# A longer booked duration for TensorE's rounded matmuls in a list scheduler's table: one layer of a hybrid Fourier, DeltaNet and ConvFFN backbone

## The chip, the cores and the metric

The kernel runs on one core of a Trainium2 chip. The core has five engines that run side by side, each with its own queue of instructions in a fixed order: TensorE (PE; its weight loads are shown apart as PEld), VectorE (DVE), ScalarE (ACT), GpSimd (POOL) and SyncE (SP), which issues all DMAs here. An instruction that depends on another engine's waits for a semaphore, and whatever stands behind it in its queue waits with it. The metric is the device time of one execution in microseconds (us), the median of several runs; lower is better.

## The reference

One layer, on 1024 latent tokens of 1024 channels with 256 context tokens, in float32:

```python
hc = modulate(rms_norm(ctx, norm_pre_mix[l]), csh1, csc1)
fc, oc, zc, gtc, ctx_states = mixer_core(hc, (zero, zero), w_in[l], ...)
hx = modulate(rms_norm(x, norm_pre_mix[l]), sh1, sc1)
fx, ox, zx, gtx, _ = mixer_core(hx, ctx_states, w_in[l], ...)
yx = merge_branches(fx, ox, zx, gtx, dn_norm[l], w_fourier[l], w_dn[l], w_out[l])
x = x + gt1 * rms_norm(yx, norm_post_mix[l])
x = ffn_sublayer(x, sh2, sc2, gt2, norm_pre_ffn[l], norm_post_ffn[l], w_up[l],
                 conv_ffn[l], w_down[l], rows, GRID_W)
```

`mixer_core` projects the tokens, applies a short depthwise convolution and SiLU to queries, keys and values, and runs a gated delta rule in chunks, forwards and backwards, for 8 heads of 128 channels; the context's final states start the latent pass. `merge_branches` takes a two-dimensional Fourier transform of 512 channels, gates both branches and projects them. `ffn_sublayer` is a ConvFFN of width 2816 with a 3x3 depthwise convolution on a grid 64 wide.

## The kernel before

**Arithmetic.** Every large product is computed from operands that are split into a rounded high part and a rounded remainder (type float32r, `F32R`): high by high, high by low, low by high (`product`, line 542). With a contraction of 1024 one half of a product, 128 rows by 512 columns, is 8 x 3 = 24 matmuls that accumulate in one PSUM bank. ScalarE makes a weight's high part and VectorE or POOL its remainder (`halves` and `split_over`, from line 526), after a DMA. Transposes and the delta rule's 128x128 products are plain float32.

**Stages.** First come the modulation rows (from `w_ada`), the pre-norms and transposes, then decay and beta. The delta-rule stage runs over ten parts, the heads x0 to x7 of the latent tokens and two groups of four context heads, c0 and c1 (`ORDER`, line 32). For each part it projects the query and convolves it (`kq_head`, `conv_taps` at line 743), forms decay products, inverts the 32x32 diagonal blocks of a triangular matrix row by row on VectorE (`invert_blocks`, line 837, 31 pairs of a multiplication and a subtraction), with round trips through DRAM, merges the blocks with small matmuls (`merge_blocks`, line 860) and scans over 8 chunks in both directions (`step`, `scan_head`). Projections that are due later (keys and values of the later heads, z, the branch gates, the Fourier input) are recorded beside them (`sides`, line 1186) with their own weight buffers and mostly one PSUM bank. Then come the Fourier transform, the remaining gates, the gated output, the projections `w_dn` and `w_fourier`, `w_out` with a norm, and the ConvFFN: `up_a` (line 1507) projects and convolves on VectorE, `up_u` projects and multiplies, `down` accumulates.

**Order.** None of this is issued as it is written. `record` (line 291) stores each operation with a booked duration from `cost` (line 247) and its dependencies; memory is laid out in fixed regions, so the reuse of a buffer or a bank is a dependency too (`gates`, line 323). `schedule` (line 351) then merges all of them once, before the program runs:

- An operation's rank is its booked duration plus the longest booked path behind it, plus a bonus that some operations have (`BON`, line 37), minus 0.1 (`MIX`) of the TensorE time booked for the operations recorded ahead of it (line 371).
- Each engine has a clock of its own in this plan. In each round the engine that can start first is taken; among its operations that are ready within 50 ns (`AHEAD`, line 27, used in line 410) the one of the highest rank is issued, and its end is its start plus the booked duration.
- A result reaches another engine after a booked latency (`LAT`, line 190, and `lat`, line 472: 200 ns from TensorE, 256 and 281 to it, 127 between two dependent operations of one engine other than TensorE, 1900 from a DMA).
- SyncE's DMAs have a booked transfer time and may run some 3 us ahead of it (`LEAD`, line 40). After a planned pause of over 3 us TensorE is booked at double durations for a while.

The order in which they come out is the order in which the instructions are written for all engines. On the chip the queues then run freely, held by semaphores alone. The booked durations decide nothing else. The profile puts nearly all instructions on line 349, the helper that issues them; groups are told apart by engine, operation and shape.

Of the kernel before, what the change touches and what calls it, by code (L numbers as in the profile page):

```python
# [10 lines left out]
F32R = mybir.dt.float32r  # L11
# [30 lines left out]
GR = T // GW  # L42


# [1 line left out]
def _groups(side):  # L46
    out, cur = [], None
    for tok in side.replace("(", " ( ").replace(")", " ) ").split():
        if tok == "(":
            cur = []  # L50
        elif tok == ")":
            out.append(cur)
            cur = None
        elif cur is None:
            out.append([tok])
        else:
            cur.append(tok)
    return out
# [130 lines left out]
class Program:  # L189
# [8 lines left out]
    def pool(self, name, bufs=1, space=None, side="left"):  # L198
        p = Pool(self, name, bufs, space, side)
        if space is None:  # L200
            self.events.append((True, p))
        return p
# [44 lines left out]
    def cost(self, eng, method, args, kw):  # L247
        out = args[0] if args else kw["out"]
        shape = out.shape
        n = math.prod(shape[1:])  # L250
        ins = [x for x in list(args[1:]) + list(kw.values()) if isinstance(x, View)]
        psum = any(v.slot.space == PSUM for v in ins)
        if eng == "PE":
            if method == "transpose":
                return max(53, args[1].shape[0] * 2 / 2.4 + 2)
            rhs, m = args[2], math.prod(args[1].shape[1:])
            n = max(math.prod(rhs.shape[1:]), m)
            if rhs.shape[0] <= 64 and m <= 64:
                return 34 if n <= 32 else 80
            return n / 2.4 + 3 if rhs.dtype == F32R and n >= 256 else n * 4 / 2.4 + 5  # L260
        if eng == "DVE":
            if method == "reciprocal":
                return 65 + 6.3 * n
            ptr = any(v.shape[-1] == 1 and v.arr.size <= P for v in ins) and method in ("tensor_scalar", "scalar_tensor_tensor")
            fast = method in ("tensor_copy", "tensor_scalar") and not psum and out.slot.space != PSUM
            return 66 + n / (1.92 if fast else 0.96) + (61 if ptr else 0)
        if eng == "ACT":
            aps = any(isinstance(kw.get(x), View) for x in ("scale", "bias", "accum_out"))
            return (51 if psum else 93) + n * 0.833 + (93 if aps else 0)
        if eng == "POOL":  # L270
            if method == "memset":
                return 36 + 0.83 * n
            if kw.get("op") == ALU.pow:
                return 300 + 165 * n
            if method == "tensor_copy":
                return 119 + 3.33 * n
            if method == "affine_select":
                return 1060
            return 140 + 2.12 * n
        run = 1  # L280
        view = out if isinstance(out, View) else args[1]
        if isinstance(view, View):
            a_ = view.arr
            for d in range(a_.ndim - 1, -1, -1):
                if a_.shape[d] > 1 and a_.strides[d] != run:
                    break
                run *= a_.shape[d]
        total = math.prod(shape) * 4
        return max(60.0, total / 359.0 * (1 if run * 4 >= 512 else 2))
# [192 lines left out]
def body(tc, a, out):  # L482
    prog = Program(tc)
    layer(prog, a, out)
    prog.run()


def layer(prog, a, out):
# [14 lines left out]
    def ps(tag, shape, name):  # L503
        return psum.tile(shape, F32, tag=tag, name=name, bufs=PPB if tag == "pp" else 1)
# [4 lines left out]
        rota[1] += 1  # L509
        return ps(rota[0][rota[1] % len(rota[0])], shape, name)  # L510

    # ---------------------------------------------------------------- constants
    prog.bonus = 2e5
    cc = cload("cc")
    ident = cload("ident", src=a["cst"][:, 0:128])
# [6 lines left out]
    po.memset(mhalf, -0.5)  # L522
    ve.tensor_scalar(convw, convw, 0.5, None, op0=ALU.mult)

    # ---------------------------------------------------------------- weights
    def halves(src, pl, tags, name, eng=None):
        n = src.shape[-1]
        h = pl.tile([P, n], F32R, tag=tags[0], name=f"h_{name}", bufs=WB[tags[0]])
        w = pl.tile([P, n], F32, tag=tags[1], name=f"w_{name}", bufs=WB[tags[1]])
        sp.dma_start(w, src)  # L530
        return h, split_over(pl, h, w, f"l_{name}", eng)
# [24 lines left out]
            (eng_h or ve).tensor_copy(h, src)  # L556
        (eng_l or ve).tensor_tensor(l, src, h.bitcast(F32), op=ALU.subtract)

    # ---------------------------------------------------------------- hidden states
    hx = pool("hx", bufs=1)  # L560

    dp = pool("delta", bufs=1, side="right")
# [6 lines left out]
    def dt(tag, name, shape=(P, T), dtype=F32):  # L569
        return dp.tile(list(shape), dtype, tag=tag, name=name, bufs=bufs.get(tag, 1))  # L570

    # ---------------------------------------------------------------- modulation, pre-norm
    prog.bonus = 2e5
    s = const.tile([P, KT, 2], F32, name="silu_c")
    th = dt("vt", "tanh_c", (P, KT, 2))
# [87 lines left out]
    def hxh(g):  # L663
        return lambda k: (hH[k][:, g * HALF:(g + 1) * HALF], hL[k][:, g * HALF:(g + 1) * HALF])

    # ---------------------------------------------------------------- decay and beta
    NCH = 10

    def small(name):
        return const.tile([P, 2, NH, NCH], F32, name=name)  # L670

    beta, ngc, eg, egl, etl = (small(n) for n in ("beta", "ngc", "eg", "egl", "etl"))
# [66 lines left out]
        for i in range(2):  # L739
            sp.dma_start(grd[80 * i:80 * i + 80, :], grs[:, i, :])  # L740

    # ---------------------------------------------------------------- conv of q, k, v
    def conv_taps(pt, acc, w3):
        n = acc.shape[-1]
        se.activation(acc, pt[:, 0:n], AF.Identity, scale=w3[:, 1:2])
        ve.scalar_tensor_tensor(acc[:, 1:n], pt[:, 0:n - 1], w3[:, 0:1], acc[:, 1:n], op0=ALU.mult, op1=ALU.add)
        ve.scalar_tensor_tensor(acc[:, 0:n - 1], pt[:, 1:n], w3[:, 2:3], acc[:, 0:n - 1], op0=ALU.mult, op1=ALU.add)
# [22 lines left out]
        ve.tensor_scalar(qn, squares(src, name, ("pd", "pd")), P * EPS, P * EPS * EPS, op0=ALU.mult, op1=ALU.add)  # L770
        return qn

    # ---------------------------------------------------------------- delta rule: preparation
    def coefs(name, rk, cols):
        b2 = const.tile([P, 2, 8], F32, tag="b2", name=f"b2_{name}", bufs=2)
        bk = const.tile([P, 2, 8], F32, tag="bk", name=f"bk_{name}", bufs=2)
        c1 = const.tile([P, 2, 8], F32, tag="c1", name=f"c1_{name}", bufs=2)
        rkb = rk.rearrange("p (o u) -> p o u", o=1).broadcast_to([P, 2, 8])
        ve.tensor_tensor(bk, cols(beta), rkb, op=ALU.mult)
        ve.tensor_tensor(b2, bk, rkb, op=ALU.mult)  # L780
        ve.scalar_tensor_tensor(c1, cols(eg), -1.0, rkb, op0=ALU.mult, op1=ALU.mult)
        return rk, b2, bk, c1
# [77 lines left out]
    def merge_blocks(name, LTs, bk, k2):  # L860
# [8 lines left out]
            po.tensor_copy(nb[bnd[b], :, bnd[b]], k1[bnd[b], NU:2 * NU, :])  # L869
        f1, f2 = k1[:, 0:NU, :], k2[:, 0:NU, :]  # L870
        b1, b2_ = k1[:, NU:2 * NU, :], k2[:, NU:2 * NU, :]
        # 32 -> 64
        pa = ps("pm", [P, NU, 32], f"pa_{name}")
        for u in range(NU):
            for q in range(2):
# [24 lines left out]
            te.matmul(pc[bnd[2], u, :], am[bnd[3], u, :], b2_[bnd[3], u, :], start=True, stop=True)  # L900
        ve.tensor_copy(Lf[bnd[1], :, bnd[0]], pc[bnd[1]])
        ve.tensor_copy(Lb[bnd[2], :, bnd[3]], pc[bnd[2]])
        # 64 -> 128
        pd_ = ps("pm", [P, NU, 64], f"pdd_{name}")
        for u in range(NU):
            te.matmul(pd_[lo64, u, :], Lf[hi64, u, lo64], nf[hi64, u, hi64], start=True, stop=True)
# [13 lines left out]

    sd_ = dram.tile([2, NH, P, P], F32, name="sdram")

    # ---------------------------------------------------------------- context pass
    def wi_k(h):
        return a["wi"][1 + 3 * h]

# [122 lines left out]
            for d in range(2):  # L1049
                sp.dma_start(sd_[d, 4 * p + hh], S[d])  # L1050

    # ---------------------------------------------------------------- latent pass
    od = dram.tile([NH, P, T], F32, name="od")
    zd = dram.tile([NH, P, T], F32, name="zd")
    rsd = dram.tile([NH, T], F32, name="rsd")
# [122 lines left out]
    @on_stage  # L1178
    def merge(i):
        co, _, fl = prep[i]  # L1180
        merged[i] = merge_blocks(stages[i][0], fl[1], co[2], blocks.pop(i))
# [53 lines left out]
            side("f", 2 * i - 16)  # L1235
            side("f", 2 * i - 15)

    # ---------------------------------------------------------------- Fourier branch
    ffd = dram.tile([NF, P, T], F32, name="ffd")
    QT = HALF // 2  # L1240
    waves = [dt("F", f"wave{e}", (P, 2, 2, QT)) for e in range(2)]
# [62 lines left out]
    close(dp)  # L1304
    rota[0] = ["pp", FBANK, "X0", "X1", "Y0", "Y1"]

    # ---------------------------------------------------------------- branch gates, gated delta output
    mp = pool("mH", bufs=17, side="right")

    def m_tile(p_, name, dtype=F32R):  # L1310
# [99 lines left out]
    close(yt)  # L1410
    close(ozp)

    # ---------------------------------------------------------------- merge of the branches
    lp = pool("mL", bufs=17, side="right")
    mH, mL = [[None] * 2 for _ in range(KT)], [[None] * 2 for _ in range(KT)]
    wop = pool("wo", bufs=1, side="right")
# [17 lines left out]
    close(gt)  # L1434
    close(fp)

    # ---------------------------------------------------------------- mixer output, second pre-norm
    x1d = dram.tile([T, D], F32, name="x1d")
    wp = pool("wp", bufs=2, side="right")
    g1r = wp.tile([P, D], F32, name="g1r", bufs=1)  # L1440
# [20 lines left out]
    for t in range(8):  # L1461
# [3 lines left out]
        n = 0  # L1465
# [23 lines left out]
    close(wp)  # L1489
    close(wop)  # L1490

    # ---------------------------------------------------------------- ConvFFN
    yp = pool("y2", bufs=1)
    y2 = [yp.tile([P, D], F32, name=f"y2_{t}") for t in range(8)]
    dwp = pool("wd", bufs=3)
# [156 lines left out]
```

## Time and profile before

| | |
|---|---|
| device time, median of 3 runs | 2151.86 us (2146.21, 2151.86, 2153.07) |
| span of the profiled execution | 2152.6 us; the profile shows no time of its own beside it |
| mean granted TensorE clock | 0.976 of full speed |
| idle time just before matmuls of the largest group | 106.2 us, of which 65.5 ended by DVE |
| DMA | 232.32 MB, mean 108 GB/s |

The span runs from the first to the last instruction. A group in the profile is one kind of instruction, with its output and input shapes, the number of its instructions, its busy time and the mean "duration" of one, and then the idle time of its engine just before them and what ended it. Matmuls are pipelined and their ends are modelled, so the mean duration of a matmul is more than its spacing in a dense stretch. The granted clock is the share of full speed that TensorE got; it falls where TensorE has stood idle.

### The profile page before, as it was taken

Reading aid. Unit: us, or ns where it says so; the run is one execution under the profiler, and the core shown is the slowest. Engines: PE = TensorE matmul, PEld = TensorE weight load, DVE = VectorE, ACT = ScalarE, POOL = GpSimd, SP = SyncE. Lnnn points to the kernel's source line nnn. Section 1 sums busy time; section 2 is a strip of 40 time slices with the busy share of each in tenths; the row PEclk is TensorE's granted clock in tenths of the full one; section 3 lists DMA queues with packets and bytes.
Section 4 is the critical chain, followed back from the end, with each engine's and each line's share of the span. In section 5 each row is a group of like instructions: output and inputs, shape, how many; then the busy total and the mean of one; then the engine's idle time right before and its main releaser. Section 6 shows DMA issues by size and latency. Waiting matters only on the chain. (4 is left out here: it accounts for less than half of the span.)

```text
span 2152.6 us, 31012 instructions
## 1 busy us (share of the span) xinstructions
PE 2023.2 (94%) x11734; PEld 1623.3 (75%) x11734; DVE 1378.7 (64%) x2608; ACT 740.5 (34%) x1740; POOL 486.8 (23%) x479
## 2 busy tenths in 40 slices
PE   6989999898979989999999999989999999999996
PEld 2777878786768777788777778768888888888885
DVE  7548767676677566653656492587465757475655
ACT  6365454453244433533421142422231222112212
POOL 4131121324233442441311000412010110101005
PEclk9999999899999999999999999989999999999998
DMA  7152323462342444332778561311111111111114
GB/s 274 47 190 83 105 84 126 130 195 66 97 134 84 120 128 114 101 105 76 230 251 292 165 220 42 105 40 44 40 59 35 54 49 45 50 45 50 49 49 147
DMA packets 164216, 232.32 MB, mean 108 GB/s; under 512 B 74097, under 2 KB 87250, under 8 KB 164066
## 3 DMA queue, kind: packets, MB, share of 16 engines
q1 hardware_dynamic: 164066, 230.34, 33.3%
q8 instruction: 92, 1.51, 0.3%
q14 instruction: 58, 0.48, 0.1%
HBM read 180.89 MB, written 49.40 MB: 107 GB/s over the span
## 5 line engine op out<-in xcount | busy, mean ns | idle before, releaser
L349 PE MATMUL p<-m,m 128*128 128x512 f32 (+5 forms) x11574 | 2009.4, 340 | 106.2 <-DVE m L349 65.5
L349 PEld LDWEIGHTS p<-m,m 128*128 128x128 f32 (+3 forms) x11574 | 1604.4, 174 | 501.6 <-ACT m L349 68.8
L349 POOL TENSOR_TENSOR m<-m,m 128x512 fp32r<-128x512 f32 (+6 forms) x244 | 380.5, 1572 | 1332.0 <-ACT m L349 532.6
L349 ACT ACTIVATE m<-m 128x512 fp32r<-128x512 f32 (+6 forms) x563 | 390.3, 711 | 775.0 <-DMA m<-in_wu_dram 254.4
L349 DVE TENSOR_TENSOR m<-m,m 128x512 fp32r<-128x512 f32 (+23 forms) x940 | 483.3, 521 | 192.7 <-ACT m L349 166.4
L349 DVE SCALAR_TENSOR_TENSOR m<-m,m,m 128x1024 f32<-128x1024 f32 (+2 forms) x260 | 304.2, 1176 | 37.8 <-DMA m<-in_w_ada_dram 24.4
L349 ACT ACTIVATE m<-p 128x128 f32<-128x128 f32 (+5 forms) x444 | 181.7, 427 | 336.9 <-PE p L349 309.2
L349 DVE SCALAR_TENSOR_TENSOR m<-p,m,m 128x128 f32<-128x128 f32 (+4 forms) x472 | 191.0, 442 | 110.3 <-ACT m L349 57.6
L349 ACT ACTIVATE m<-p,m 128x128 f32<-128x128 f32 (+2 forms) x240 | 115.6, 492 | 235.8 <-PE p L349 219.8
L349 DVE TENSOR_TENSOR m<-m,p 128x512 f32<-128x512 f32 (+3 forms) x229 | 123.8, 569 | 105.9 <-PE p L349 105.8
L349 DVE SCALAR_TENSOR_TENSOR m<-m,m 128x512 f32<-128x512 f32 (+6 forms) x141 | 107.0, 768 | 36.6 <-ACT m L349 29.1
L349 DVE COPY m<-p 32x256 f32<-32x256 f32 (+10 forms) x116 | 42.0, 367 | 64.0 <-ACT m L349 38.5
L349 POOL COPY m<-m 32x256 f32<-32x256 f32 (+2 forms) x136 | 53.6, 397 | 115.3 <-DMA m<-d 73.5
L349 DVE SCALAR_TENSOR_TENSOR m<-m,m,p 128x128 f32<-128x128 f32 x128 | 42.8, 342 | 41.5 <-PE p L349 40.2
L349 DVE TENSOR_SCALAR m<-m,m 128x1024 f32<-128x1024 f32 x44 | 35.2, 799 | 49.1 <-ACT m L349 36.0
L349 POOL MEMSET m<- 128x1024 f32 (+7 forms) x79 | 35.1, 456 | 134.9 <-PE p L349 101.6
L349 ACT ACTIVATE p<-p 128x128 f32<-128x128 f32 x208 | 55.3, 266 | 20.6 <-PE p L349 18.6
L349 DVE STREAM_TRANSPOSE m<-m 32x256 f32<-32x256 f32 (+1 forms) x50 | 24.5, 491 | 29.1 <-DMA m<-d 28.4
L349 DVE CAST m<-m 128x512 fp32r<-128x512 f32 (+3 forms) x45 | 26.3, 593 | 25.0 <-ACT m L349 23.4
L349 ACT ACTIVATION_READ_ACCUMULATOR p<-p 128x1 f32 x208 | 40.0, 192 | 0.0
L349 DVE TENSOR_TENSOR m<-p,m 128x512 f32<-128x512 f32 (+4 forms) x47 | 28.1, 608 | 11.9 <-PE p L349 11.7
L349 POOL TENSOR_SCALAR_AFFINE_SELECT m<-m 128x1024 f32<-128x1024 f32 x16 | 19.0, 1207 | 72.2 <-DVE m L349 72.2
(20 smaller groups left out, 130.4 us busy)
## 6 DMA issues: line engine op xcount, KB each, us to landing
m<-d SPq DMA_DIRECT2D x76, 512.0 KB
m<-d SPq DMA_DIRECT2D x114, 256.0 KB
m<-in_wi_dram SPq DMA_DIRECT2D x106, 256.0 KB
m<-in_w_ada_dram SPq DMA_DIRECT2D x48, 512.0 KB
d<-m SPq DMA_DIRECT2D x94, 256.0 KB
m<-in_wu_dram SPq DMA_DIRECT2D x88, 256.0 KB
m<-in_wn_dram SPq DMA_DIRECT2D x22, 512.0 KB
m<-in_x_dram SPq DMA_DIRECT2D x16, 512.0 KB
```

The source lines that it names most:

```text
L349: return getattr(engine.real, method)(*[real(v) for v in args], **{k_: real(v) for k_, v in kw.items()})
```

## The change

In `cost`, the booked duration of a TensorE matmul on rounded operands with 256 columns or more is longer: n/2.4 + 16 ns instead of n/2.4 + 3 for more than 256 columns, n/2.4 + 12 for 256. A plain float32 matmul is booked 1 ns longer. Nothing else is different but comment lines that became blank; all line numbers stay. What is computed, the instructions, the tiles, the buffers and the DMAs are the same, and `schedule` merges them anew with these numbers.

```diff
@@ -257,7 +257,7 @@
             n = max(math.prod(rhs.shape[1:]), m)
             if rhs.shape[0] <= 64 and m <= 64:
                 return 34 if n <= 32 else 80
-            return n / 2.4 + 3 if rhs.dtype == F32R and n >= 256 else n * 4 / 2.4 + 5
+            return n / 2.4 + (16 if n > 256 else 12) if rhs.dtype == F32R and n >= 256 else n * 4 / 2.4 + 6
         if eng == "DVE":
             if method == "reciprocal":
                 return 65 + 6.3 * n
```

## The prediction

> **What bounds the kernel now.** I read the page's head and its slices first, then the table of windows by stage, the chain of waits, TensorE's waits in the one stage that has many, and the timeline where the longest of them lie.
>
> ```profile
> span 2152.6 us, 31012 instructions
> PE 2023.2 (94%) x11734; PEld 1623.3 (75%) x11734; DVE 1378.7 (64%) x2608; ACT 740.5 (34%) x1740; POOL 486.8 (23%) x479
> ```
>
> TensorE (PE) is busy for 94% of the span, so 2152.6 - 2023.2 = 129.4 us are all that any order could win back from its idle time. The table of windows says where they lie; I cut it at the ends of the stages.
>
> ```profile
> 0.00:160.00 160.00, 130.59 (x639) 94.51 (x640) 97.77 (x180) 90.75 (x206) 54.16 (x54) 0.94 0.48 172
> 160.00:1000.00 840.00, 773.86 (x6271) 641.06 (x6270) 572.65 (x1586) 367.98 (x1058) 261.49 (x295) 0.97 0.37 110
> 1000.00:1380.00 380.00, 376.70 (x1655) 293.43 (x1654) 215.17 (x326) 106.67 (x204) 59.78 (x54) 1.00 0.55 185
> 1380.00:1440.00 60.00, 49.87 (x196) 36.53 (x195) 43.70 (x42) 18.92 (x27) 17.21 (x12) 0.89 0.16 54
> 1440.00:2123.00 683.00, 683.00 (x2940) 550.59 (x2939) 429.96 (x451) 150.93 (x230) 79.01 (x53) 1.00 0.15 49
> 2123.00:2153.00 30.00, 9.19 (x41) 7.17 (x39) 19.45 (x24) 5.24 (x16) 15.17 (x14) 0.69 0.50 175
> ```
>
> The columns after the length are busy time of PE, PEld, DVE, ACT and POOL, then the granted clock, the DMA share and GB/s. The loading of the first weights (0 to 160) leaves PE idle for 29.4 us, the delta-rule stage (160 to 1000) for 66.1 us, the start of the ConvFFN (1380 to 1440) for 10.1 us, the tail behind the last matmuls for 20.8 us. From 1440 to 2123 it is never idle. The clock was granted at 0.97 in the delta-rule stage, another 0.03 x 840 = 25 us at most. So about 66 + 25 = 91 us lie where an order has choices. The chain of waits gives the true spacing of the matmuls that the change books:
>
> ```profile
> 1655.63 100.66 PE p L349 x432
> 1756.30 100.43 PE p L349 x432
> ```
>
> 432 of them in 100.43 us are **232.5 ns** apiece, with nothing in between. The mean "duration" of the same group (below, 419 ns) overlaps its neighbours and isn't a spacing.
>
> **The change, part by part.** Line 260 books a rounded matmul of 512 columns at 512/2.4 + 3 = 216.3 ns; after it, at 512/2.4 + 16 = 229.3, 13.0 more. One of 256 columns goes from 109.7 to 118.7 (+9.0); a plain fp32 one gains 1 ns. No instruction is added, removed or reshaped: the 31012 stay, with their DMAs. What moves is the merge of the five queues.
>
> ```profile
> L349 PE MATMUL p<-m,m 128*128 128x512 f32 x1826 | 534.4, 419 | 22.8 <-DVE m L349 15.2 <-ACT m L349 6.8 <-ACT p L349 0.2
> L349 PE MATMUL p<-m,m 128*128 128x256 f32 x264 | 46.5, 303 | 4.4 <-DVE m L349 3.8 <-ACT m L349 0.4
> ```
>
> These are the groups of 160 to 1000. The plan's TensorE takes 1826 x 13.0 + 264 x 9.0 = 23.7 + 2.4 = 26 us longer over this stage than it did. On the chip nothing is longer. Two things change in line 351's merge. First the ranks: each half of a product (24 matmuls) on an operation's longest path raises it by 24 x 13.0 = 0.31 us, and the charge for lateness, 0.1 of the TensorE time recorded before it (line 371), grows as well. Only pairs of ready operations whose ranks lay that close change places. Second, the clock of the plan: at each product the other engines' operations seem ready earlier against TensorE than they did.
>
> Before, the plan's TensorE ran ahead of the chip's by 232.5 - 216.3 = 16.2 ns a matmul, 16.2 x 1826 = 29.6 us over the stage; after, by 232.5 - 229.3 = 3.2 ns, 5.8 us. **The change removes 23.8 us of this lag** of the chip behind its plan. What the lag does is seen in the engines that wait, in order, for PE's products (same window):
>
> ```profile
> DVE m L349 <- PE p L349: 112.0, 104, 4.4
> DVE m L349 <- ACT m L349: 87.0, 50, 7.7
> DVE m L349 <- DMA m<-d: 33.7, 12, 6.8
> DVE m L349 <- ACT p L349: 13.0, 6, 5.1
> DVE m L349 <- DMA d<-m: 4.2, 2, 3.9
> PE p L349 <- DVE m L349: 43.9, 34, 6.5
> PE p L349 <- ACT m L349: 12.6, 12, 4.8
> PE p L349 <- DMA m<-d: 6.1, 3, 5.3
> ```
>
> VectorE stands waiting 249.9 us, of which 112.0 (45%) for a matmul; what is queued behind the waiting instruction can't start, though its inputs may be there, and PE in turn waits 43.9 us for VectorE. A plan that has the end of a product right puts fewer such instructions too early. The gain lies between nothing (all lag hidden, since PE is busy for 92% of the stage) and the whole 23.8 us. I take VectorE's share: 0.45 x 23.8 = 10.7 us, an estimate.
>
> The other stages I cost at nothing. From 1440 on, PE is full and VectorE covers the rest with 430 of 683 us; if a conv came too late there, the nearest row is the wait at the ConvFFN's start, 4.94 us:
>
> ```profile
> 1427.14 3.32 PE L349 MATMUL p<-m,m 128*128 128x512 f32 x7 [4.94 <-DVE m L349]
> SPq L349 <- PE p L349: 1168.3, 266, 26.2
> ```
>
> That wait ends with the first conv and hangs on data; it stays, as do the loads at the start and the tail. SP's queue, too, is merged anew: its booked transfer times are unchanged, so in the plan loads come earlier against PE. On the chip most of them wait for PE to free a buffer (1168.3 us of waiting), which a booking doesn't hasten; the two or three buffers of each weight tag are the cover. If a load stood behind the wrong wait, the nearest row is PE's 5.28 us for a DMA, shown below; I take zero.
>
> By the Trainium skill ("TensorE: Matmul & The Clock Gate", section "Back-to-back issue gap") an isolated warm matmul of N columns is spaced N/2.4 + 2.5 ns, 215.8 for 512, and it gives some 131 as sustained. By either the old booking was right or long, and the new one is wrong by 13.5 ns or more. The trace disagrees with 232.5 ns over 864 matmuls.
>
> Sum: 2152.6 - 10.7 = 2141.9. The profile shows no time of that execution beside its span; the span lies 0.7 us over the median, 2151.86, well inside the runs (2146.21 to 2153.07), so I carry the difference over: 2151.86 - 10.7 = **2141** us.
>
> **The rivals.** *VectorE is planned too early (slower).* The longest wait of the delta-rule stage:
>
> ```profile
> 486.94 7.31 DVE L349 TENSOR_TENSOR m<-m,m 128x121 f32<-128x121 f32 x17
> 487.06 4.22 POOL L349 TENSOR_TENSOR m<-m,m 128x8 f32<-128x8 f32 x2 [0.98 <-DVE m L349]
> 491.52 0.67 ACT L349 ACTIVATE m<-p,m 128x512 f32<-128x512 f32 x1
> 494.28 2.87 DVE L349 TENSOR_TENSOR m<-m,m 128x30 f32<-128x30 f32 x4
> 497.07 0.74 DVE L349 SCALAR_TENSOR_TENSOR m<-p,m,m 128x511 f32<-128x511 f32 x1
> 498.74 3.75 PE L349 MATMUL p<-m,m 128*128 128x512 f32 x8 [6.52 <-DVE m L349]
> 480.00:500.00 20.00, 10.80 (x50) 8.27 (x51) 18.54 (x37) 12.24 (x40) 10.45 (x5) 0.91 0.34 118
> 500.00:520.00 20.00, 20.00 (x282) 15.23 (x282) 7.98 (x17) 6.73 (x13) 9.56 (x17) 0.92 0.34 97
> ```
>
> ScalarE had evacuated the product by 492.2; the conv taps on VectorE (128x511, line 743), which free its bank, came at 497.07, behind rows of the block inversion (line 837), and PE stood for 6.52 us. The granted clock of the two slices fell to 0.91 and 0.92, another (0.09 + 0.08) x 20 = 3.4 us: 9.9 us for one such block. The plan's longer product leaves room for more of these rows ahead of the taps: one is booked at 66 + 121/0.96 + 127 = 319 ns, and the half-product just grew by 312. And the rows run late:
>
> ```profile
> 623.72 1.78 DVE L349 TENSOR_TENSOR m<-m,m 128x121 f32<-128x121 f32 x5
> 627.61 10.21 DVE L349 TENSOR_TENSOR m<-m,m 128x78 f32<-128x78 f32 x11
> 627.74 10.04 POOL L349 TENSOR_TENSOR m<-m,m 128x8 f32<-128x8 f32 x5 [4.52 <-DVE m L349]
> 645.89 4.30 PE L349 MATMUL p<-m,m 32*32 32x32 f32 x70 [5.28 <-DMA m<-d]
> ```
>
> Five take 356 ns apiece with POOL quiet, eleven 928 ns apiece beside POOL. So where a row more falls beside POOL, the taps slip by up to 0.9 us. The rival decides once more than one new block of 9.9 us appears, net of the gain, in the ten stages of the scan; at three new ones less the gain, +29.7 - 10.7 = +19.0, it gives 2171 us. Against it: the same rows alone are near their booking, and only products lengthen in the plan. The Trainium skill ("SBUF — State Buffer", section "Who interferes with whom") has a VectorE operation with two SBUF inputs and a GpSimd one that reads SBUF block each other for a whole instruction; the 928 against 356 ns agree, and by it the late rows are a fixture wherever POOL works.
>
> *The waits hang on data (no change).* The 5.28 us above end with the inverse's round trip through DRAM, the 4.94 with the first conv, and the stage has as much work for PE after as before; losses move from one head to another and their sum holds. That gives 2152 us, within 6.5. It is also the outcome if few ranks lay close enough to flip.
>
> *The old booking was the better one.* If products in the stage were spaced as booked before, the new plan's TensorE would run 13.0 x 1826 = 23.7 us behind the chip's, and by the same share cost 0.45 x 23.7 = 10.7: 2163 us. The skill's isolated gap would make it so; the row of 232.5 speaks against it, and it holds little chance.
>
> **How the numbers follow.** About 0.3% (6.5 us) is what a measurement of this kernel can tell from no change. Forecast, faster: 0.42. Waits that hang on data: 0.27. VectorE too early: 0.30. Old booking better: 0.01. Hence faster 0.42, same 0.27, slower 0.31; time 2141. The likeliest case alone runs from 2128 (all 23.8 us) to 2145. The waits of the stage can be dealt better than the lag accounts for: 91 us are there, and four blocks less of 9.9 reach 2112. On the slow side the rival's 2171 with half a block more reaches 2176. Range 2112 to 2176; 1 in 10 left out at either end.
>
> **What would show it.** If the steps hold: 432 matmuls of the dense part still in about 100.5 us; PE's idle time in the delta-rule stage down from 66 to some 55 us; VectorE's wait for PE under 112; the last stages unchanged to 2 us. If VectorE is too early: PE's waits for DVE above 43.9 us, more of them over 4 us ended by 128x511 taps, clocks of 0.9 in more slices. If only shifted: other places, same sum. The forecast is wrong if VectorE's wait for PE falls and PE's idle time doesn't, or if the loss lies past 1000 us.

## The result, and the profile after

The changed kernel takes **2162.4 us** (median of 5, 2159.84 to 2173.77) against 2151.86 before: 1.0061 times as long, 95% interval 1.0047 to 1.0075. It is slower by some 10 us by the medians, where 2141 was forecast. The profiled execution took 2159.84 us, the shortest of the five, of which 1.7 lie around its span; so the two profiles differ by 5.5 us of span, not by the 10 of the medians.

The head of the page after the change (busy time and share of the span of each engine):

```profile
span 2158.1 us, 31050 instructions
PE 2028.2 (94%) x11734; PEld 1625.6 (75%) x11734; DVE 1379.0 (64%) x2608; ACT 737.7 (34%) x1740; POOL 485.3 (22%) x479
```

The five engines' counts are those of before to the last instruction; the 38 more in the total are of the kinds that the page counts as no work. So only the order changed. The table of windows after the change, cut at the same times (columns as in the prediction):

```profile
0.00:160.00 160.00, 133.75 (x662) 99.36 (x663) 102.22 (x192) 95.02 (x211) 54.22 (x55) 0.94 0.49 173
160.00:1000.00 840.00, 769.31 (x6214) 634.04 (x6213) 564.36 (x1572) 361.20 (x1052) 262.00 (x293) 0.96 0.37 109
1000.00:1380.00 380.00, 373.45 (x1643) 292.21 (x1643) 212.85 (x317) 102.56 (x196) 56.36 (x49) 1.00 0.55 182
1380.00:1440.00 60.00, 50.42 (x212) 36.41 (x211) 47.53 (x51) 21.86 (x34) 21.38 (x16) 0.97 0.24 79
1440.00:2123.00 683.00, 683.00 (x2931) 549.16 (x2930) 428.29 (x447) 149.10 (x224) 72.19 (x49) 1.00 0.15 47
2123.00:2158.00 35.00, 18.27 (x79) 14.39 (x77) 23.75 (x33) 7.92 (x24) 19.12 (x18) 0.81 0.61 210
```

PE's idle time in the delta-rule stage (160 to 1000) rose from 66.1 to 840 - 769.31 = 70.7 us, and from 1000 to 1380 from 3.3 to 6.55. Busy time alone misleads here, though: a matmul's record is longer than its spacing. A surer measure is how many products of 512 columns are done by a given time, at 232.5 ns each (the prediction's spacing). The largest group of PE in the windows 0 to 1000 and 0 to 1440, before:

```profile
L349 PE MATMUL p<-m,m 128*128 128x512 f32 x2099 | 609.0, 419 | 24.9 <-DVE m L349 16.3 <-ACT m L349 6.8 <-ACT p L349 1.1
...
L349 PE MATMUL p<-m,m 128*128 128x512 f32 x3694 | 997.3, 411 | 37.4 <-DVE m L349 23.8 <-ACT m L349 8.8 <-POOL m L349 2.9
```

and after:

```profile
L349 PE MATMUL p<-m,m 128*128 128x512 f32 x2082 | 610.9, 420 | 38.7 <-DVE m L349 26.5 <-ACT m L349 10.0 <-ACT p L349 1.4
...
L349 PE MATMUL p<-m,m 128*128 128x512 f32 x3665 | 993.8, 411 | 50.6 <-DVE m L349 35.9 <-ACT m L349 10.8 <-POOL m L349 1.8
```

By 1000 us the new order is 17 products (4.0 us) behind, by 1440 it is 29 (6.7 us); at 160 it had been 15 ahead (290 against 275). So the delta-rule stage lost 32 products or 7.4 us, 1000 to 1440 another 12 or 2.8 (most of this belongs to the stage, too: by 1000 us 16 matmuls of 128x128 fewer are done as well, 1878 for 1894, 1.8 us at their spacing of 111 ns), and the ConvFFN's 683 us hold 2931 matmuls where they held 2940, 2.1 us. The tail gave about 4 back: PE's idle time behind 2123 fell from 20.8 to 16.7 us.

The prediction's witness, VectorE's wait for PE, did not move. Waits of the delta-rule stage after the change (total, times, longest), VectorE's first and then TensorE's:

```profile
DVE m L349 <- PE p L349: 113.6, 108, 5.1
...
PE p L349 <- DVE m L349: 39.9, 27, 7.5
PE p L349 <- ACT m L349: 17.2, 12, 7.7
PE p L349 <- DMA m<-d: 6.6, 5, 2.1
```

112.0 before, 113.6 after. PE's wait for VectorE even fell (43.9 to 39.9), and that for ScalarE rose (12.6 to 17.2). Some long waits do look like the first rival's. The timeline after the change, engines in order of time (a row goes on through instructions of one kind until the engine pauses, and bears the shape of the first):

```profile
545.64 4.54 PE L349 MATMUL p<-m,m 128*128 128x512 f32 x19
...
547.44 0.69 ACT L349 ACTIVATE m<-p,m 128x512 f32<-128x512 f32 x1 [3.92 <-PE p L349]
...
550.82 2.60 DVE L349 TENSOR_TENSOR m<-m,m 128x110 f32<-128x110 f32 x8
553.34 0.75 DVE L349 SCALAR_TENSOR_TENSOR m<-p,m,m 128x511 f32<-128x511 f32 x1
...
554.19 0.75 DVE L349 SCALAR_TENSOR_TENSOR m<-p,m,m 128x511 f32<-128x511 f32 x1
...
555.30 3.33 PE L349 MATMUL p<-m,m 128*128 128x512 f32 x7 [5.12 <-DVE m L349]
```

ScalarE had evacuated the product at 548.1, the convolution's taps (128x511) came at 553.3 behind rows of the inversion, and PE stood for 5.12 us. Waits of PE over 4 us are four before (23.0 us together) and five after (30.4 us). Three of the five end with such taps, one of the four did; the two longest, 7.72 and 7.45 us, do not.

### The profile page after: what moved, and what is told of

Same layout as the page of the kernel before. It is cut to its first block, busy times and chain, and to the rows that moved or that the text cites. A ratio compares the mean times of both kernels' runs of the same rounds, so it can differ in the third digit from the quotient of the medians.

```text
span 2158.1 us, 31050 instructions
## 1 busy us (share of the span) xinstructions
PE 2028.2 (94%) x11734; PEld 1625.6 (75%) x11734; DVE 1379.0 (64%) x2608; ACT 737.7 (34%) x1740; POOL 485.3 (22%) x479
## 5 line engine op out<-in xcount | busy, mean ns | idle before, releaser
L349 PEld LDWEIGHTS p<-m,m 128*128 128x128 f32 (+3 forms) x11574 | 1607.5, 175 | 510.6 <-ACT m L349 70.7
L349 DVE TENSOR_TENSOR m<-m,m 128x512 fp32r<-128x512 f32 (+21 forms) x940 | 481.8, 519 | 226.8 <-ACT m L349 193.8
L349 DVE SCALAR_TENSOR_TENSOR m<-p,m,m 128x128 f32<-128x128 f32 (+4 forms) x472 | 192.1, 441 | 111.6 <-ACT m L349 52.6
L349 DVE SCALAR_TENSOR_TENSOR m<-m,m 128x512 f32<-128x512 f32 (+6 forms) x141 | 99.8, 717 | 43.7 <-ACT m L349 33.9
L349 DVE COPY m<-p 32x256 f32<-32x256 f32 (+10 forms) x116 | 42.1, 367 | 57.3 <-ACT m L349 35.2
L349 DVE SCALAR_TENSOR_TENSOR m<-m 128x1 f32<-128x1 f32 (+1 forms) x17 | 6.4, 379 | 46.4 <-ACT m L349 44.5
L349 POOL TENSOR_SCALAR_AFFINE_SELECT m<-m 128x1024 f32<-128x1024 f32 x16 | 18.3, 1168 | 72.0 <-DVE m L349 72.0
L349 DVE CAST m<-m 128x512 fp32r<-128x512 f32 (+3 forms) x45 | 24.5, 554 | 13.5 <-ACT m L349 9.5
```

What stands on the lines that cost most here:

```text
L349: return getattr(engine.real, method)(*[real(v) for v in args], **{k_: real(v) for k_, v in kw.items()})
```

## The experiments

All 18 kernels compute the whole layer; they differ in bookings or in the merge alone, and so in the order. Each ratio is to the kernel before, which had medians of 2149.6 to 2152.0 us beside them. In the short diffs the line before is

```python
return n / 2.4 + 3 if rhs.dtype == F32R and n >= 256 else n * 4 / 2.4 + 5
```

and "A/B, F" stands for `n / 2.4 + (A if n > 256 else B)` with `n * 4 / 2.4 + F`. The kernel before is 3/3, 5, the change 16/12, 6.

**Does the length matter, or is it the luck of one order?** One theory: the longer booking itself costs time, so every order made with it is slower. Its rival: any other number in the table deals the order anew, and this deal was a bad one. The first kernel takes the fp32 part of the change alone, the next three vary the length, and the last four repeat both lengths with harmless variations of the plain fp32 booking.

3/3, 6 (the fp32 part of the change alone):

> The kernel before with only the plain fp32 matmul booked 1 ns longer (6 for 5); the rounded ones as before. Theory A (less slack: a longer booking of the rounded matmuls lets the plan put VectorE's inversion rows ahead of the conv taps, so products wait for their bank): nothing of that is touched, ratio 1.000 within 0.002, waits of products for a bank that taps hold near 22 us in the stage of 160 to 1000 us. Theory B (a new deal: any small change of booking reorders the stage, and the sum of the waits is drawn anew, without a direction): it may land anywhere from 0.993 to 1.007, as far off as the change itself.

-10/-6, 5:

> Rounded matmuls booked 13 ns shorter than before (n/2.4 - 10; 9 shorter at 256 columns), the opposite dose of the change. Theory A: more slack, so faster by about what the change cost, ratio 0.994 (some 2139 us), tap waits well under 22 us. Theory B: anywhere from 0.993 to 1.007 with no bond to the sign of the dose.

9.5/7.5, 5:

> Half the dose of the change (n/2.4 + 9.5; 7.5 at 256 columns; fp32 as before). Theory A: half the cost, ratio 1.003 (some 2158 us), tap waits between 22 and 32 us. Theory B: anywhere from 0.993 to 1.007, not in between.

30/22, 5:

> Twice the dose of the change (n/2.4 + 30; 22 at 256 columns; fp32 as before). Theory A: twice the cost, ratio 1.012 (some 2175 us), tap waits above 32 us. Theory B: anywhere from 0.993 to 1.007, as likely under the change as above it.

16/12, 5 (the rounded part of the change alone):

> The change without its extra ns on plain fp32 matmuls (rounded ones at n/2.4 + 16 and + 12, fp32 as before): the change's main part alone, and a second draw at its dose. Theory A' (the dose itself costs: with rounded matmuls booked at what they take, the plan has no slack left for what it underrates, on top of a scatter of some 5 us from one order to the next): 2157 to 2168 us, ratio 1.003 to 1.008. Theory B (the change was one unlucky draw of some 10 us either way): anywhere from 2140 to 2168, with half a chance of being under 2154.

16/12, 7:

> The change with plain fp32 booked one ns longer still (7 for 6): a third draw at the change's dose. Theory A': 2157 to 2168 us, ratio 1.003 to 1.008. Theory B: anywhere from 2140 to 2168, half a chance of under 2154.

3/3, 5.5:

> The old dose of the rounded matmuls, plain fp32 at 5.5 for 5: a third draw at the old dose (before 2152 us, e1_f32_only 2141). Theory A': 2139 to 2155 us, ratio 0.994 to 1.001. Theory B: anywhere from 2140 to 2168, half a chance of over 2154.

3/3, 4.5:

> The old dose of the rounded matmuls, plain fp32 at 4.5 for 5: a fourth draw at the old dose. Theory A': 2139 to 2155 us, ratio 0.994 to 1.001. Theory B: anywhere from 2140 to 2168, half a chance of over 2154.

The last two columns are counts: the matmuls from 1440 to 2090 us (table of windows), and the places from 160 to 1000 us where PE passes between matmuls on 32 or 64 rows and columns and wider ones (counted over the records of the trace).

| booked | us | ratio, 95% | 1440-2090 | passages |
|---|---|---|---|---|
| -10/-6, 5 | 2155.2 | 1.0016 [1.0007, 1.0025] | 2806 | 124 |
| 3/3, 4.5 | 2148.2 | 0.9984 [0.9975, 0.9993] | 2798 | 118 |
| 3/3, 5 (before) | 2151.9 | 1 | 2797 | 136 |
| 3/3, 5.5 | 2143.7 | 0.9967 [0.9955, 0.9980] | 2798 | 130 |
| 3/3, 6 | 2141.3 | 0.9949 [0.9936, 0.9962] | 2798 | 124 |
| 9.5/7.5, 5 | 2162.2 | 1.0046 [1.0030, 1.0062] | 2784 | 144 |
| 16/12, 5 | 2157.9 | 1.0034 [1.0022, 1.0047] | 2786 | 156 |
| 16/12, 6 (the change) | 2162.4 | 1.0061 [1.0047, 1.0075] | 2789 | 166 |
| 16/12, 7 | 2160.8 | 1.0045 [1.0033, 1.0058] | 2790 | 162 |
| 30/22, 5 | 2187.7 | 1.0165 [1.0152, 1.0178] | 2725 | 196 |

Both are true. One ns on the fp32 booking moves the time by half a per cent; that is the luck of an order, some 10 us. But the four orders at the old length (mean ratio 0.9975) and the three at the new one (mean 1.0047) don't overlap: the longer booking itself costs about 0.7%, some 15 us, and 30/22 costs 36. These orders are not wholly independent draws: the change and 16/12, 7 share waits (5.07 and 5.08 us near 196 us, 7.72 and 7.11 near 630), and so do 3/3, 5.5 and 3/3, 6 (9.11 and 8.92 near 500). Two more orders at each length, below, point the same way. Nor does the cost grow evenly with the length: 9.5/7.5, half the change, costs in its one order as much as the whole. Nor is it a matter of truth: 16/12 books 229.3 ns where the chip needs 232.5 and is worse than 216.3; an order from still shorter products (-10/-6) gains nothing.

**Where the plan uses the length.** One kernel puts the long booking into the ranks alone: 16/12, 5, and the added time taken off again behind line 372, where the ranks are done. The other puts it into the plan's clocks alone: 3/3, 5, with `+=` at that place.

```diff
+        for o in ops:
+            if o.eng == "PE" and o.method == "matmul" and o.args[2].dtype == F32R:
+                n = max(math.prod(o.args[2].shape[1:]), math.prod(o.args[1].shape[1:]))
+                o.cost -= 13 if n > 256 else 9
```

> Rounded matmuls booked longer (n/2.4 + 16, + 12) while the ranks are computed, and as before while the engines' clocks run in the merge. If the cost of the longer booking comes through the plan's clock (slack lost), this lies with the four at the old dose, 2140 to 2152 us. If it comes through the ranks (another priority between products and the scan), it lies with the three at the change's dose, 2157 to 2163 us.

> The reverse: ranks as before, rounded matmuls booked longer only while the engines' clocks run in the merge. Slack lost: 2157 to 2163 us. Ranks: 2140 to 2152 us.

Ranks alone: 2152.4 us, 1.0001 [0.9989, 1.0014], 132 passages, 2795 matmuls from 1440 to 2090. Clocks alone: 2158.1 us, 1.0032 [1.0020, 1.0044], 176 and 2782. By the total it is one order each, within luck; by these two counts the clock carries the effect. The count of 512-column products done by 1440 us does not tell them apart: 3673 with ranks alone (in the slowest of its runs, which is the one profiled) and 3663 with clocks alone, both under the four at the old length (3694 to 3747). So for the delta-rule stage it stays open which of the two carries the loss.

**Rows of the inversion booked too short?** The prediction had seen rows of 356 to 928 ns beside a booking of 319. Perhaps short products were the slack for them. (The 928 is the mean of a mixed row: seven of the eleven instructions took 0.21 to 0.29 us, and four, each beside one POOL instruction of 1024 columns, 1.8 to 2.3.) Booked 100 ns longer, with the change and without it:

```diff
-            return 66 + n / (1.92 if fast else 0.96) + (61 if ptr else 0)
+            row = 100 if method == "tensor_tensor" and n <= 144 and not psum else 0
+            return 66 + n / (1.92 if fast else 0.96) + (61 if ptr else 0) + row
```

> The change, and VectorE's small products and differences of two SBUF operands (144 columns at most, the inversion rows above all) booked 100 ns longer, about what they take on the chip beside POOL. Theory C (the slack was needed for the rows, which the plan has too short, so that conv taps come late): the cost is gone, 2140 to 2150 us, and PE's wait for DVE in 160 to 1000 us falls from 40 to under 30 us. Theory D (slack is needed at every hand-over of a bank, on ScalarE and in the ConvFFN too): no more than a few us of it come back, 2154 to 2166 us.

> The kernel before with the rows booked 100 ns longer. Theory C: faster than the four at the old dose, 2132 to 2142 us, PE's wait for DVE under 35 us where it was 38 to 45. Theory D: within their scatter, 2140 to 2152 us.

With the change 2175.8 us (1.0116 [1.0103, 1.0129]), without it 2183.3 (1.0153 [1.0140, 1.0166]): both much slower. TensorE's waits in the delta-rule stage of the first (one line was added, so L350):

```profile
PE p L350 <- DVE m L350: 30.0, 28, 4.5
PE p L350 <- DMA m<-d: 23.8, 8, 7.7
PE p L350 <- ACT m L350: 23.7, 22, 3.7
```

The wait for VectorE fell as meant (39.9 to 30.0), but that for the inverse's round trip rose from 6.6 to 23.8 and that for ScalarE from 17.2 to 23.7. So this booking doesn't pay, but it is a blunt test: of the stage's 638 operations of this kind (144 columns at most, two SBUF operands) before the change 29 took over 1 us and the others 0.29 on average, close to their booking with the 127 ns; 100 ns were put on all of them. That the few held rows matter is not refuted by it; their number does not follow the length, though (29, 21, 24 and 22 at the old one, 26, 27 and 25 at the new).

**Split groups and hand-overs.** Two things that the trace shows and the table books at nothing are left. First, the passages of the last column rise with the booked length, 127 on average at the old one, 161 at the new. Among `merge_blocks`' 64-row matmuls after the change, PE's weight loads in order of time:

```profile
859.86 1.73 PEld L349 LDWEIGHTS p<-m,m 128*128 128x128 f32 x12
861.86 0.67 PEld L349 LDWEIGHTS p<-m,m 64*64 64x64 f32 x5 [0.28 <-issue]
862.76 1.23 PEld L349 LDWEIGHTS p<-m,m 64*64 64x64 f32 x10 [0.23 <-issue]
864.35 1.23 PEld L349 LDWEIGHTS p<-m,m 64*64 64x64 f32 x10 [0.35 <-issue]
865.94 0.67 PEld L349 LDWEIGHTS p<-m,m 64*64 64x64 f32 x7 [0.36 <-issue]
866.86 0.44 PEld L349 LDWEIGHTS p<-m,m 64*64 64x64 f32 x3 [0.24 <-issue]
867.54 0.45 PEld L349 LDWEIGHTS p<-m,m 64*64 64x64 f32 x5 [0.24 <-issue]
```

A row is not one shape here: it begins with two or four 64-row loads and goes on with wide ones. By the single records, 32 loads of 64 rows between 861.86 and 869.84 come in eleven pieces of two or four, with one to three loads of products behind each but the last. Over the delta-rule stage, a passage costs 0.11 to 0.12 us (14.3 us for 127 before, 18.3 for 155 after: from start to start, less the usual spacing of the first matmul's shape, gaps of 0.3 us and more above it left out). Second, the reuse of a PSUM bank goes through `gates`, booked at latency 0, while the chip needs 53 to 147 ns from the evacuating instruction's end to the next matmul's start where PE waits for it. A half-product booked 24 x 13.0 = 312 ns shorter may have hidden that. One kernel keeps small matmuls together as long as any is ready, one books the hand-over, one does both; all with the change's lengths (16/12, 6). The first edit stands behind line 413 (`n` is the engine taken, `o` the operation, `last` PE's operation before it, and `small` a matmul on at most 64 rows and columns); it puts `o` back and takes the highest-ranked of `more`:

```diff
+            if n == "PE" and small(last) and not small(o):
+                more = [e for e in can[n] if small(e[2])]
+                if more:
```

The second is at lines 328 and 474:

```diff
-            g, r = Op(), slot.region
+            g, r = Op(method="bank" if slot.space == PSUM else None), slot.region
-            return 0.0
+            return 170.0 if q.method == "bank" and o.eng in ("ACT", "DVE") else 0.0
```

> The change, with one rule more in the merge: after a small matmul (32 or 64 rows and columns, the merging of blocks) another ready small one goes before anything else on PE. The plan's times are the same to the last digit; PE changes between small and other matmuls 118 times for 166. In the traces so far such a passage costs some 0.115 us beyond the matmuls (18.5 us for 155 of them between 160 and 1000 us at the change's dose, 12.8 for 117 at the old one). Theory S (the longer booking costs by splitting these groups): 48 x 0.115 = 5.5 us come back, 2150 to 2157 us by the mean of that dose (2160) less 5.5. Rival (the passages are an effect without a price, the time goes to waits): 2157 to 2163 us.

> The change, with 170 ns booked between VectorE's or ScalarE's last use of a PSUM bank and the matmul that reuses it, where the plan books nothing (the chip shows 53 to 147 ns from the end of the record to the matmul's start, at a wait). Theory D (the short booking gave 24 x 13 ns a half-product of slack, which covered this hand-over): most of what waits at the hand-overs comes back, the ConvFFN's 3.7 us among it, 2148 to 2155 us; passages between small and other matmuls are 134 too. Rival (a booked hand-over only deals anew): 2156 to 2165 us.

> Both together: the change, small matmuls kept together (116 passages) and 170 ns booked for the hand-over of a bank. Theories S and D: back at the four of the old dose, 2141 to 2152 us. Neither: 2156 to 2165 us.

The counter-tests put both edits on the old length (3/3 with fp32 6, and with 5, which is the kernel before), and on the new one with fp32 5:

> e1_f32_only (the old dose, plain fp32 one ns longer, 2141 us) with both additions. Its passages fall only from 124 to 120, and its slack was there already. Theories S and D: little to win, 2136 to 2146 us. If a booked hand-over costs by leaving PE idle in the plan, as the longer rows did: 2150 us and more.

> The kernel before (plain fp32 at 5 ns) with both additions: a second draw of e16_old_both. If the two additions are worth some 14 us at the old dose, 2130 to 2142 us. If e16 was a lucky order, 2142 to 2152 us.

> The longer booking of the rounded matmuls alone (as e5_rounded_only) with both additions: a second draw of e15_change_both. If the dose costs even with groups kept together and hand-overs booked, 2145 to 2156 us, over e16 and e17. If these two were all that it cost, no more than 5 us over the mean of e16 and e17.

| booked, with | us | ratio, 95% | 1440-2090 | passages |
|---|---|---|---|---|
| 16/12, 6, kept together | 2156.9 | 1.0048 [1.0031, 1.0066] | 2789 | 118 |
| 16/12, 6, hand-over | 2155.6 | 1.0023 [1.0012, 1.0033] | 2798 | 134 |
| 16/12, 6, both | 2149.1 | 1.0001 [0.9993, 1.0010] | 2798 | 116 |
| 16/12, 5, both | 2153.8 | 1.0009 [0.9997, 1.0022] | 2800 | 116 |
| 3/3, 6, both | **2127.6** | 0.9900 [0.9887, 0.9912] | 2802 | 120 |
| 3/3, 5, both | 2133.4 | 0.9920 [0.9903, 0.9936] | 2801 | 116 |

The ConvFFN is settled. Its table of windows shows a PE that is never idle, and yet more or fewer matmuls of one shape in the same 650 us. Before:

```profile
1440.00:2090.00 650.00, 650.00 (x2797) 523.64 (x2796) 416.18 (x430) 143.63 (x212) 65.00 (x40) 1.00 0.15 47
```

After the change:

```profile
1440.00:2090.00 650.00, 650.00 (x2789) 522.42 (x2788) 415.01 (x427) 141.89 (x210) 61.00 (x39) 1.00 0.15 46
```

With the change and the hand-over booked:

```profile
1440.00:2090.00 650.00, 650.00 (x2798) 523.41 (x2798) 412.07 (x425) 142.07 (x211) 60.04 (x38) 1.00 0.15 47
```

The four orders at 3/3 of the first table have 2797 or 2798, those at 16/12 2786 to 2790, those at 16/12 with the hand-over booked 2798 to 2800; keeping groups together changes nothing here (2789). The single records, which the views merge, show where the time goes. Two matmuls of this shape start 231 ns apart (median). In each of the four orders at the old length, 4 matmuls of these 650 us start over 350 ns after the one ahead, and 52 to 54 ns behind the end of a ScalarE instruction that reads PSUM (that it empties their bank is inferred); their spacing and the next one are up to 399 and 340 ns, some 0.27 us lost each time. At the new length there are 13 or 14 of them, with ranks alone 1, with clocks alone 18, and with the change and the hand-over booked none. Ten more at some 0.26 us are 2.6 us. So the 2 us that this stage lost are hand-overs that the short booking had kept apart.

The split groups are shown in the delta-rule stage. The 64-row matmuls' group there (busy time, mean ns of one, then idle time before), before:

```profile
L349 PE MATMUL p<-m,m 64*64 64x64 f32 x640 | 28.2, 232 | 3.1 <-ACT m L349 1.7 <-DVE m L349 1.1 <-issue 0.3
```

After the change:

```profile
L349 PE MATMUL p<-m,m 64*64 64x64 f32 x640 | 30.7, 233 | 2.1 <-DVE m L349 1.2 <-ACT m L349 0.9
```

With the change and groups kept together:

```profile
L349 PE MATMUL p<-m,m 64*64 64x64 f32 x640 | 25.1, 229 | 2.6 <-DVE m L349 1.8 <-ACT m L349 0.8
```

The group's busy time, 28.2 before, 30.7 after and 25.1 with 48 passages fewer, follows the split. The timeline of PE's weight loads with groups kept together has the like in two rows; by the single records each is 32 loads of 64 rows in one piece, then wide ones (26 in the first):

```profile
851.37 4.90 PEld L349 LDWEIGHTS p<-m,m 64*64 64x64 f32 x58 [0.41 <-issue]
856.54 5.30 PEld L349 LDWEIGHTS p<-m,m 64*64 64x64 f32 x55 [0.27 <-issue]
```

The total of this kernel, 5.5 us under the change's by the medians but 2.8 by the ratios (1.0048 and 1.0061, each to the kernel before beside it), has an interval that overlaps with the change's; the passages are gone for certain, the gain in time less so. With the hand-over alone booked the passages fell as well, from 166 to 134, so outside the ConvFFN its 2155.6 us can't be put to the hand-over alone. By the Trainium skill ("TensorEngine Tiling (Array Packing)", section "Key Properties") a change of the tiling mode drains TensorE; the 0.11 to 0.12 us a passage agree with that (that the mode changes there is read off the shapes), and the section has no price for it.

What these two do **not** explain is the gap itself. With both booked, the new length stands at 2149.1 and 2153.8, the old at 2127.6 and 2133.4: still some 20 us apart, at the same number of passages and nearly the same ConvFFN. The gap lies before 1440: by then the order on 16/12, 6 has done 3689 products, that on 3/3, 6 3816 of them, 127 x 232.5 ns = 29.5 us. The window of the delta-rule stage of the first, and TensorE's waits there:

```profile
160.00:1000.00 840.00, 764.85 (x6248) 635.31 (x6247) 564.49 (x1575) 361.80 (x1052) 260.27 (x293) 0.96 0.37 109
```

```profile
PE p L349 <- DVE m L349: 42.1, 32, 8.3
PE p L349 <- ACT m L349: 16.3, 13, 5.6
PE p L349 <- DMA m<-d: 14.4, 7, 9.3
```

The same of the second:

```profile
160.00:1000.00 840.00, 786.37 (x6386) 656.51 (x6385) 563.85 (x1604) 374.09 (x1080) 264.15 (x297) 0.97 0.38 112
```

```profile
PE p L349 <- DVE m L349: 28.6, 26, 7.2
PE p L349 <- ACT m L349: 14.1, 12, 6.3
PE p L349 <- DMA m<-d: 4.9, 6, 1.7
```

On the longer booking PE waits 13.5 us more for VectorE and 9.5 more for DMAs (the other pair: 42.7 against 35.2, and 18.4 against 5.4). All of PE's waits in the stage come to 73.7 and 78.3 us at the new length and 52.3 and 64.2 at the old one, 17.8 us more on average: most of the 20. Some 7 of these are one wait: near 943 us PE stands 9.31 and 9.18 us for the round trip of an inverse, where the longest wait for a DMA at the old length is 1.70 and 2.21. It comes with the hand-over booked at the new length (9.37 us with that alone) and not with the change by itself (2.06), so it need not be an effect of the length. Why a plan with longer products makes the other waits is **open**; no run here takes it apart. The old length with both edits was thought to have little left to win; at 3/3, 6 it won 13.7 us on the same length without them, at 3/3, 5 18.5 (by the ratios 0.5% and 0.8%). Which of the two edits won it was not tried at the old length. Both orders beat the two kernels of this study, the faster at 0.9900 of the time before.

## Why the prediction was wrong, point by point

- **The size of the edit** was right: no instruction became longer, the dense spacing stayed (2798 of one shape in 650 us are 232.3 ns apiece, 2789 are 233.1), and the plan's TensorE does run closer to the chip's. The stage itself has the same spacing (median 231 ns). The old booking was not the better description; the rival "the old booking was the better one" is refuted as it was put, and that its price, +10.7, is close to what happened is luck.
- **The step that failed**: "A plan that has the end of a product right puts fewer such instructions too early", with the term 0.45 x 23.8 = 10.7 us. VectorE's wait for PE is 112.0, 117.7, 109.6 and 111.6 us in the four orders at the old length and 113.6, 110.3 and 122.6 at the new one: nothing was won. The lag of 23.8 us was treated as an error to be removed. In the ConvFFN the runs show that it was slack: it stood in for hand-overs of a bank that the table books at nothing (4 late starts before, 14 after, none with the hand-over booked). In the delta-rule stage its going brought more passages, through the plan's clocks as far as one order each can tell, and more waits for ScalarE; by what step the plan comes to split the groups and to wait was not taken apart, and the larger part of the loss stays open.
- **"The other stages I cost at nothing"** failed as well. Over the orders at both lengths, counted in 512-column products at 232.5 ns, the new length is on average 14 ahead at 160 us (3.3 us won), 30 behind at 1000 and 46 behind at 1440: 44 products or 10.3 us lost in the delta-rule stage, 16 or 3.8 us from 1000 to 1440, and 9.4 matmuls or 2.2 us in the ConvFFN, "PE is full" or not. (By 1000 us 14 matmuls of 128x128 fewer are done, too, on average, 1.6 us, so that much of the 3.8 belongs to the delta-rule stage.) A busy PE was taken for a PE at its pace; the two rows of 432 matmuls "with nothing in between" begin at such late starts, 1655.63 and 1756.30 us. Part of it comes back in the tail: the profiled spans differ by 10.3 us on average (2145.8 and 2156.1). "The last stages unchanged to 2 us" missed by little, and for a cause that the prediction didn't have.
- **The delta-rule stage's 10.3 us** on average: 34 more passages at 0.11 to 0.12 us are some 3.9; PE's waits, all releasers summed, rose from 60.7 to 66.5, which are 5.8. Within them those for VectorE fell (41.8 to 35.5), those for ScalarE rose (10.9 to 18.7). Idle time from 66 to 55 was forecast; it became 70.7.
- **The rival "VectorE is planned too early"** had the sign, and the waits behind inversion rows that it described are there one by one (5.12 us above; three over 4 us for one before), but not its main sign: PE's wait for VectorE should have passed 43.9 us and is 39.9, and lower still in the other two orders at this length (36.4, 30.1). Its price, 19 us for three new blocks of 9.9, was double what came. It is not what the longer booking does systematically. Its reading of the rows was off as well: they do not slip by 0.9 us beside POOL, but in the row shown four are held for 1.8 to 2.3 us and the other seven take 0.21 to 0.29.
- **"Waits hang on data"** (2152) was refuted by the interval of the ratio, though only by some 10 us, about the spread between orders at one length. The prediction had no term for this spread: a one-ns change elsewhere in the table moved the kernel by -0.5%, as much as the whole gain that was forecast.
- By the Trainium skill ("TensorE: Matmul & The Clock Gate", section "Back-to-back issue gap") an isolated warm matmul of 512 columns is spaced 215.8 ns from the next; the dense stretches here give 232 to 233. The length of before, 216.3, is nearer to the Trainium skill's figure and served better, but not as a truth of the chip.

## What to carry to other kernels

When a booking in a planner's table proves wrong, ask what else it pays for before you correct it: hand-overs and passages that are booked at zero may live in its error. Book the missing costs first and try the corrected length by itself: here the two edits together gained 0.8% on the kernel before, and the truer length lost with them and without. And judge such a change by several orders per setting (vary a harmless number) and by counts at fixed times, for one order carries half a per cent of luck in it.

## What the runs showed of the hardware

- A passage between matmuls on 32 or 64 rows and columns and wider ones costs 0.11 to 0.12 us beyond the spacing of the first (0.11 by the median when the small ones end, 0.09 when they begin).
- A PE that the profile shows as never idle still loses time at hand-overs of a PSUM bank, 0.26 to 0.27 us each in the ConvFFN: 2784 to 2806 matmuls of one shape in the same 650 us by order alone, with 0.02 us of idle time at most (30/22 apart, whose 2725 have 6.7 us of it).
- A VectorE row of two SBUF operands is held for nearly as long as the POOL instruction beside it: before the change, from 629.5 to 638 us, four rows of 16 or 30 columns take 1.8 to 2.3 us beside POOL instructions of 1.9 to 2.4 us on 1024 columns, while the seven rows ahead of them take 0.21 to 0.29.
